# RMS norm and projection on one core: another list schedule for the first six tiles, with earlier and later loads, transposes and casts

The kernel runs on one core of one Trainium2 chip. The metric is device time in microseconds (us) of one execution; lower is better. The kernel before takes 388.32 us (median of three runs, 387.97 to 388.36).

## The reference

```python
# x: 8 x 1024 x 768 f32, gamma: 768, w_qkv: 768 x 2304, eps: 1e-5
rms = np.sqrt(np.mean(x ** 2, axis=-1, keepdims=True) + eps)
x_norm = x / rms * gamma
return np.matmul(x_norm, w_qkv).astype(np.float32)
```

The 8,192 rows of x are 64 tiles of 128 rows. Each tile is multiplied with the whole weight: 6 slices of the contraction (k = 0 to 5) times 2,304 output columns.

## The kernel before

Gamma is folded into the weights as they are cast to bf16 (`conv`). A tile of x is cast, transposed, and multiplied; 1/rms is applied when a result leaves PSUM (`evac`). Tiles 0 to 2 are transposed by TensorE straight from f32 (`trA`, `trB`: slices 0 to 3 and 4 to 5), tile 3 from bf16 (`tr`), and all later ones by the DMA crossbar (`xbar`). In the head (tiles 0 to 5) the weights are still arriving, in 16 pieces. A plan that a list scheduler wrote earlier holds a time for each operation, and only the order within each engine's stream comes out of these times.

```python
PIECES = [(0, 2, 0, 512), (2, 3, 0, 512), (3, 4, 0, 512), ...]   # k0, k1, first column, columns

LOADS = [
    (-9.00, "w", 0), (-8.99, "x", 0), (-8.98, "x", 1), (-8.97, "x", 2), (-8.96, "w", 1),
    (-8.95, "w", 2), (-8.94, "w", 3), (-8.93, "x", 3), (-8.92, "w", 4), (-8.91, "w", 5),
    ...                                          # "t" n: crossbar transpose of tile n
    (15.55, "w", 13), (22.65, "t", 5), ...
]
HEAD_PLAN = [
    (4.98, "conv", 0, 0, "DVE"), (5.46, "conv", 0, 1, "DVE"), (5.94, "trA", 0), (5.98, "stat", 0),
    ...
]
...
    PIECE_BUFS = {(k1 - k0, n): min(4, sum(...)) for k0, k1, _, n in PIECES}   # buffers of a shape
...
    def xbar(t):
        XT[t] = xTp.tile([P, KO, P], bf16, name="xT")
        nc.sync.dma_start_transpose(out=XT[t], in_=XB[t])
...
    at(0.0, idle, 5, NT)          # filler matmuls before the first tile
    at(2.8, gamma_in)
    at(2.81, idle, 6, NT)
...
    for _, _, fn, args in sorted(plan, key=lambda p: p[:2]):
        fn(*args)
```

All loads (but that of gamma), stores and crossbar transposes are issued by SyncE, so they stand in one queue in this order. Tiles 6 to 63 follow from a loop that the change does not touch.

## Time and profile before

| of the kernel before | value |
|---|---|
| time, median of three | 388.32 us |
| span of the profiled execution | 386.2 us |
| TensorE busy | 379.2 us (98%) |
| chain that ended last: share of TensorE | 91% |
| first real matmul starts | 7.53 us |
| tile 5's transpose lands, TensorE goes on | 28.54, 28.58 us |
| last matmul starts | 382.50 us |

Times of the trace count from the span's start. "Landing" is the time at which a load's completion semaphore is full, in the trace's records. TensorE's matmuls overlap, so its real losses are read from start to start: a 512-wide bf16 matmul takes 0.2158 us that way, though the profile shows 0.38 for one alone.

### The profile page before, as it was taken

To read this page: it belongs to the slowest core of one execution; us is meant where nothing else is said; L and a number is where in the kernel's file an instruction comes from. 1 tells how busy PE (TensorE), PEld (TensorE's weight loads), DVE (VectorE), ACT (ScalarE), POOL (GpSimd) and SP (SyncE) were. 2 spreads that over 40 slices of the span, in tenths; PEclk is the share of its full clock that TensorE was granted. 3 is DMA by queue.
4 is the path that set the end of the run, shared out by engine and by line. 5 is a ranking of instruction groups with operands and counts; after the bars stand their busy time and mean duration, and the time that the engine had idled before them with its cause. 6 is when DMAs were issued, how large, how long until landed. Compare 5 with 4: busy or idle time off the path is not lost.

```text
span 386.2 us, 5458 instructions
## 1 busy us (share of the span) xinstructions
PE 379.2 (98%) x1921; PEld 191.5 (50%) x1959; DVE 153.1 (40%) x307; ACT 181.5 (47%) x365; POOL 6.6 (2%) x14
## 2 busy tenths in 40 slices
PE   8999999999999999999999999999999999999996
PEld 4444655455454454554554554554554554554553
DVE  3744433433333344333344333343333343333332
ACT  5752644453544443544444444544444534444532
POOL 0130000000000000000000000000000000000000
PEclk9999999999999999999999999999999999999999
DMA  8999999999999999999999999999999999999995
GB/s 289 391 296 401 401 318 358 321 367 305 331 293 306 310 284 328 294 291 325 276 319 316 298 297 311 299 311 263 297 358 290 306 311 285 290 326 314 282 269 191
DMA packets 89575, 119.91 MB, mean 310 GB/s; under 512 B 52422, under 2 KB 61388, under 8 KB 89548
## 3 DMA queue, kind: packets, MB, share of 16 engines
q1 hardware_dynamic: 89536, 119.56, 101.5%
q8 instruction: 15, 0.25, 0.3%
q14 instruction: 12, 0.10, 0.1%
q10 hardware_dynamic: 12, 0.00, 0.0%
HBM read 32.25 MB, written 75.50 MB: 279 GB/s over the span
## 4 chain that ended last, share of the span: by engine, by line
PE 91%; DMA 6%; issue 1%; DVE 0%; ACT 0%; SPq 0%; DVEq 0%
PE pm L234 91%; DMA x_t<-in_x_dram 3%; DMA w_f<-in_w_qkv_dram 2%; DMA xT<-xb 2%; ACT ot L253 0%; DVE ot L251 0%; DVE xb L174 0%; SPq L160 0%; SPq L155 0%; DVEq L356 0%; ACT w_b L168 0%
## 5 line engine op out<-in xcount | busy, mean ns | idle before, releaser
L234 PE MATMUL pm<-w_b,xT 128*128 128x512 bf16 (+1 forms) x1882 | 372.1, 357 | 2.2 <-DMA xT<-xb 0.2
L234 PEld LDWEIGHTS <-xT 128*128 128x128 bf16 x1920 | 187.7, 98 | 185.6 <-DMA xT<-xb 0.7
L253 ACT ACTIVATE ot<-pm,rstd 128x512 f32<-128x512 f32 (+2 forms) x160 | 102.8, 644 | 192.3 <-PE pm L234 154.5
L251 DVE TENSOR_SCALAR ot<-pm,rstd 128x512 f32<-128x512 f32 (+1 forms) x161 | 111.3, 694 | 201.7 <-PE pm L234 199.1
L185 ACT ACTIVATE sq<-x_t 128x768 bf16<-128x768 f32 x64 | 53.3, 834 | 3.2 <-DMA x_t<-in_x_dram 3.2
L174 DVE CAST xb<-x_t 128x768 bf16<-128x768 f32 x61 | 33.2, 545 | 18.4 <-DMA x_t<-in_x_dram 18.2
L187 ACT ACTIVATE rms<-ssq,eps_sb 128x1 f32<-128x1 f32 x64 | 18.9, 295 | 2.1
L185 ACT ACTIVATION_READ_ACCUMULATOR sq<-x_t 128x1 f32 x64 | 12.2, 191 | 0.0
L166 DVE TENSOR_SCALAR w_b<-w_f,g_sb 128x512 bf16<-128x512 f32 (+1 forms) x16 | 7.7, 499 | 6.3 <-DMA w_f<-in_w_qkv_dram 6.3
L192 DVE RECIPROCAL rstd<-rms 128x1 f32<-128x1 f32 x64 | 9.8, 153 | 0.0
L170 POOL TENSOR_SCALAR w_b<-w_f,g_sb 128x512 bf16<-128x512 f32 (+1 forms) x8 | 5.9, 739 | 23.1 <-DMA w_f<-in_w_qkv_dram 23.1
L286 PE MATMUL pm<-const-float32-0.0 128*128 128x512 bf16 (+1 forms) x14 | 4.8, 491 | 0.8 <-PEq L342 0.8
L168 ACT ACTIVATE w_b<-w_f,g_sb 128x512 bf16<-128x512 f32 (+1 forms) x6 | 3.6, 612 | 2.9 <-DMA w_f<-in_w_qkv_dram 2.9
L212 PE MATMUL pm<-ident_f,x_t 128*128 128x128 f32 x18 | 2.6, 279 | 0.6 <-DMA x_t<-in_x_dram 0.5
L286 PEld LDWEIGHTS <-const-float32-0.0 128*128 128x128 bf16 x14 | 1.5, 123 | 2.6 <-issue 2.6
L212 PEld LDWEIGHTS pm<-ident_f,x_t 128*128 128x128 f32 x18 | 1.9, 140 | 1.6 <-DMA x_t<-in_x_dram 1.3
L176 ACT CAST xT<-pm 128x256 bf16<-128x256 f32 (+1 forms) x5 | 2.2, 454 | 0.2
L142 ACT ACT_TABLE_LOAD x1 | 1.3, 1283 | 1.4 <-PEq L342 1.4
L174 DVE CAST xT<-pm 128x512 bf16<-128x512 f32 x1 | 0.7, 690 | 0.7 <-PE pm L212 0.7
L269 DVE COPY g_sb<-pm 128x6 f32<-128x6 f32 x1 | 0.2, 165 | 1.7 <-PE pm L268 1.7
L268 PEld LDWEIGHTS pm<-ident_f,g 6*128 6x128 f32 x1 | 0.2, 177 | 0.8 <-issue 0.8
L174 DVE COPY xT<-pm 128x768 bf16<-128x768 bf16 x1 | 0.6, 557 | 0.0
(12 smaller groups left out, 2.5 us busy)
## 6 DMA issues: line engine op xcount, KB each, us to landing
out_dram<-ot SPq DMA_DIRECT2D x124, 512.0 KB, 3.9
x_t<-in_x_dram SPq DMA_DIRECT2D x64, 384.0 KB, 4.3
out_dram<-ot SPq DMA_DIRECT2D x64, 128.0 KB, 3.2
w_f<-in_w_qkv_dram SPq DMA_DIRECT2D x10, 512.0 KB, 7.5
out_dram<-ot SPq DMA_DIRECT2D x8, 256.0 KB, 2.0
w_f<-in_w_qkv_dram SPq DMA_DIRECT2D x4, 256.0 KB, 5.8
xT<-xb SPq DMA_TRANSPOSE x60, 4.3
w_f<-in_w_qkv_dram SPq DMA_DIRECT2D x2, 384.0 KB, 5.9
```

What stands on the lines that cost most here:

```text
L166: nc.vector.tensor_scalar(out=o, in0=i, scalar1=g, scalar2=None, op0=mult)
L168: nc.scalar.activation(out=o, in_=i, func=AF.Copy, scale=g, bias=0.0)
L170: nc.gpsimd.tensor_scalar(out=o, in0=i, scalar1=g, scalar2=1.0, op0=mult, op1=mult)
L174: nc.vector.tensor_copy(out=out, in_=in_)
L185: nc.scalar.activation(out=sq, in_=X[t], func=AF.Square, accum_out=ssq)
L187: nc.scalar.activation(out=rms, in_=ssq, func=AF.Sqrt, scale=inv_k, bias=eps_sb)
L192: nc.vector.reciprocal(out=r, in_=RS[t])
L212: nc.tensor.transpose(out=PT[t, h][:, ko - k0, :], in_=X[t][:, ko * P:(ko + 1) * P], identity=ident_f)
L234: nc.tensor.matmul(out=PM[t, n0][:, :nl], lhsT=XT[t][:, ko, :], rhs=w_b[:, ko, n0:n0 + nl], start=(b == 1), stop=(b == KO))
L251: nc.vector.tensor_scalar(out=o[:, :d], in0=pm[:, :d], scalar1=RS[t], scalar2=None, op0=mult)
L253: nc.scalar.activation(out=o[:, d:], in_=pm[:, d:nl], func=AF.Copy, scale=RS[t], bias=0.0)
L286: nc.tensor.matmul(out=wps[:, :nl], lhsT=zeros[:, :P], rhs=zeros[:, :nl], start=True, stop=True)
```

## The change

The intent is a shorter head from another run of the list scheduler. In the head the order on every engine changes, and for some casts, copies and evictions the engine too; the work stays the same but for three filler matmuls. The core of the diff:

```diff
 LOADS = [
     (-9.00, "w", 0), (-8.99, "x", 0), (-8.98, "x", 1), (-8.97, "x", 2), (-8.96, "w", 1),
-    (-8.95, "w", 2), (-8.94, "w", 3), (-8.93, "x", 3), (-8.92, "w", 4), (-8.91, "w", 5),
-    (-8.90, "w", 6), (-8.89, "x", 4), (-8.88, "w", 7), (-8.87, "w", 8), (-8.86, "w", 9),
-    (-8.85, "w", 10), (-8.84, "x", 5), (15.52, "t", 4), (15.53, "w", 11), (15.54, "w", 12),
-    (15.55, "w", 13), (22.65, "t", 5), (22.66, "w", 14), (22.67, "w", 15), (22.68, "x", 6),
-    (22.69, "x", 7),
+    (-8.95, "w", 2), (-8.94, "x", 3), (-8.93, "w", 3), (-8.92, "w", 4), (-8.91, "w", 5),
+    (-8.90, "w", 6), (-8.89, "w", 7), (-8.88, "x", 4), (-8.87, "w", 8), (-8.86, "w", 9),
+    (-8.85, "w", 10), (-8.84, "x", 5), (16.68, "t", 4), (16.69, "w", 11), (16.70, "w", 12),
+    (21.70, "t", 5), (21.71, "w", 13), (21.72, "w", 14), (21.73, "w", 15), (21.74, "x", 6),
+    (21.75, "x", 7),
 ]
 HEAD_PLAN = [
-    (4.98, "conv", 0, 0, "DVE"), (5.46, "conv", 0, 1, "DVE"), (5.94, "trA", 0), (5.98, "stat", 0),
-    (6.81, "trB", 0), (6.95, "cpA", 0, "DVE"), (7.03, "trB", 1), (7.24, "trA", 1),
-    (7.31, "cpB", 0, "ACT"), (7.63, "recip", 0), (7.67, "cpB", 1, "ACT"),
-    (7.69, "mm", 0, 0, "01"), (8.03, "cpA", 1, "ACT"), (8.12, "trB", 2), (8.34, "trA", 2),
...
-    (11.52, "recip", 1), (11.63, "tr", 3), (11.63, "idle", 3), (11.68, "conv", 4, 5, "DVE"),
...
+    (4.98, "conv", 0, 0, "POOL"), (4.98, "conv", 0, 1, "DVE"), (5.94, "trA", 0),
+    (5.98, "stat", 0), (6.81, "trB", 0), (7.03, "trA", 1), (7.17, "cpB", 0, "DVE"),
+    (7.31, "cpA", 0, "ACT"), (7.46, "trB", 1), (7.57, "recip", 0), (7.73, "cpA", 1, "DVE"),
+    (7.93, "trA", 2), (7.97, "stat", 2), (8.36, "mm", 0, 0, "01"), (8.64, "conv", 1, 2, "DVE"),
...
+    (10.74, "mm", 1, 0, "3"), (10.96, "tr", 3), (10.97, "conv", 3, 4, "DVE"),
+    (11.29, "mm", 2, 0, "3"), (11.45, "cp", 3, "DVE"), (11.51, "mm", 0, 0, "4"),
+    (11.64, "conv", 4, 5, "POOL"), ...
 ]
-HEAD_END = 43.99
+HEAD_END = 43.93
```

In SyncE's queue, tile 3's load moves ahead of weight piece 3, tile 4's load behind piece 7, and tile 5's transpose ahead of piece 13.

## The prediction

> **What bounds the kernel now.** I read the page first, then TensorE's waits in the first 48 us, then TensorE and its weight loads in order of time, then the DMA issues and the windows around the crossbar transposes.
>
> ```profile
> PE 379.2 (98%) x1921; PEld 191.5 (50%) x1959; DVE 153.1 (40%) x307; ACT 181.5 (47%) x365; POOL 6.6 (2%) x14
> ...
> PE 91%; DMA 6%; issue 1%; DVE 0%; ACT 0%; SPq 0%; DVEq 0%
> ```
> TensorE is busy 98% of a span of 386.2 us, and the chain that ended last is TensorE for 91%. The chain leaves TensorE only before 28.58 us and in the last 4 us; in between are nothing but groups of up to 63 matmuls with 0.05 us of issue. So the change, all of it in the head, can be worth only what TensorE loses before 28.58.
>
> ```profile
> PE pm L286 <- PEq L342: 0.8, 1, 0.8
> PE pm L212 <- DMA x_t<-in_x_dram: 0.5, 1, 0.5
> PE pm L234 <- DMA xT<-xb: 0.2, 1, 0.2
> ```
> These are all the waits of TensorE there: the start, the first tile of x, and the transpose of tile 5. Matmul ends are modelled, so smaller losses must be read from starts:
>
> ```profile
> 5.84 1.85 PE L212 MATMUL pm<-ident_f,x_t 128*128 128x128 f32 x12 [0.49 <-DMA x_t<-in_x_dram]
> 7.53 0.59 PE L234 MATMUL pm<-w_b,xT 128*128 128x512 bf16 x2
> 7.97 0.82 PE L212 MATMUL pm<-ident_f,x_t 128*128 128x128 f32 x6
> 8.62 2.97 PE L234 MATMUL pm<-w_b,xT 128*128 128x512 bf16 x13
> 11.46 0.51 PE L198 MATMUL pm<-ident,xb 128*128 128x128 bf16 x6
> 11.81 0.34 PE L286 MATMUL pm<-const-float32-0.0 128*128 128x128 bf16 x3
> 12.06 16.35 PE L234 MATMUL pm<-w_b,xT 128*128 128x512 bf16 x73
> 28.58 1.69 PE L234 MATMUL pm<-w_b,xT 128*128 128x512 bf16 x7 [0.17 <-DMA xT<-xb]
> ```
> Start to start in the trace's records, a 512-wide matmul takes 0.2158 us, an f32 transpose 0.109 (0.164 for the first after a wait) and a bf16 transpose 0.056. The 13 matmuls from 8.62 take 2.81 us, so they run gapless to 11.43. From 12.06 the program has 75 matmuls before tile 5 (73 are recorded), 16.19 us, so slots end at 28.25, but the next starts at 28.58. That wait is really 0.33 us, not 0.17.
>
> ```profile
> 26.30:27.30 1.00, 1.00 (x6) 0.49 (x5) 0.49 (x1) 0.68 (x1) 1.00 (x2) 1.00 0.07 25
> ```
> This window has start:end, length, busy time of PE, PEld, DVE, ACT and POOL, granted clock, DMA share and GB/s. Here, in the middle of tile 5's transpose, the DMA engines are almost still. In the packet records 15 of 16 rings have done half the transpose at 26.2 and wait for one that is some 18 packets of 2,048 B behind, at 84 ns each; all go on at 27.67. At 22.25 one engine had moved a 16,384-byte packet of instructions (1.09 us). The transpose, which lands at 28.54, is thus late through the load ahead of it and through one late ring.
>
> **What the Trainium skill says.** "Runtime: NRT & Kernel Launch", Instruction fetch mechanics: instructions are refilled in 16 KiB blocks of 256. The trace agrees: 15 such packets, some 24 us apart. "DMA: Bandwidth & Descriptors", Queues, rings and completion order: each issuing engine has one ring on each of the same 16 engines, with descriptors consumed in ring order. The trace agrees in effect: loads land in issue order, one 512 KB weight piece every 1.35 us and one tile of x every 0.98. "GPSIMD Engine Reference", Elementwise side-by-side: GpSimd was measured 1.96 times as slow as VectorE on an f32 add. Here a 128x512 cast takes 0.69 us on GpSimd (up to 0.99 beside VectorE) and 0.49 on VectorE, so 1.4 to 2 times. "TensorE: Matmul & The Clock Gate", Parts 1 and 4: a clock gate watches a window of about 3.4 us and may not count transposes as work. No trace here shows a drop between 4.6 and 386 us; it is a rival below.
>
> **The change part by part.** I place the new order on the landings and durations above. Loads up to the fourth tile keep their landings: first weight piece 4.83, tiles 0 to 2 at 5.80, 6.78, 7.78, next pieces 8.44 and 9.17. A matmul may start about 0.04 us after what it waits for.
>
> *Start, loses.* TensorE now does 16 transposes before any matmul. The first 12 end at 7.53 as now, but then it needs tile 2, landed at 7.78, where before two matmuls filled that time. It starts at 7.82: 0.29 lost, and 0.055 for the slow first transpose, +0.345 us. First matmul: 7.82 + 0.164 + 3 x 0.109 = 8.32. GpSimd's cast of half the first piece (ready by about 5.9) and ScalarE's copy of tile 0 (6.99 + 0.59 = 7.58) are long done, so moving the cast to GpSimd is worth nothing.
>
> *Middle, gains.* Now, 11.43 to 12.06 holds 6 bf16 transposes (0.346) and 0.29 us of three filler matmuls, the wait for the fourth tile's cast (10.85 to 11.41) and that for the fifth piece's cast, which queues behind it on VectorE. With the fourth tile a piece sooner it lands at 9.17 + 0.98 = 10.16 and its cast ends at 10.74. Counting forward from 8.32: four matmuls to 9.18 (second piece cast by 8.95), two to 9.61, two transposes to 9.83, five matmuls to 10.91, tile 3's transposes at 10.91 (cast ready, 10.78) to 11.25, one matmul to 11.47 (fourth piece, landed 10.82, cast by 11.37). Then eight matmuls while GpSimd casts the fifth piece (11.58 to 12.3 at most 12.6; needed at 13.20), and four more to 14.06. The same point is 14.00 now. So -0.29 us, and start and middle sum to +0.055.
>
> *Up to tile 5, neutral.* From 14.06 TensorE needs each weight piece at these times: sixth 14.06 (both VectorE casts done 13.8), seventh 15.79 and 16.43 (GpSimd 15.3 and at worst 16.2), eighth 17.51 (16.5), ninth 19.24 (19.0 at worst), tenth 20.96 (20.1), eleventh 22.69 (21.7). None is late, but the margins are 0.2 to 1.0 us. Tile 4's transpose is issued about a microsecond later, after a cast ending near 17.1, but still queues behind tile 5's load: landing near 22.4, needed at 23.77.
>
> *Tile 5, gains.* Its transpose now stands ahead of a 512 KB piece instead of behind it, so it lands near 28.54 - 1.35 = 27.2 even with the same late ring. TensorE reaches it at 14.06 + 66 x 0.2158 = 28.30. The wait goes: -0.33 us against a start kept at 28.25 + 0.055. The displaced piece lands near 28.5 and is needed only after 37.
>
> Sum: +0.345 - 0.29 - 0.33 = -0.275. The start at 28.58 becomes 28.30 and the rest is unchanged: 388.32 - 0.28 = 388.04, say 388.05 us. The kernel's own plan shortens by 0.06 us, as its end goes from 43.99 to 43.93; it does not know the late ring.
>
> **Rivals.** (1) *A new wait in the head.* VectorE's 0.04-us margin at tile 3's transposes and the fourth piece (0.1 us) could miss, and GpSimd's pieces could be late if its casts stretch past the 0.99 us seen. For it: seven casts of the first eleven pieces on GpSimd against four. Against: each margin is kept with worst observed durations. It would cost 0.1 to 0.7 us: 388.2 to 388.7. (2) *Tile 5 stays late.* If the fetch or the transpose's own issue (1.58 us after the cast at 22.16) delays it by 1.1 us beyond my estimate, the wait returns: about 388.4. For it: the late ring depends on when TensorE's block is fetched. Against: other transposes land a median 4.3 us after issue, so 26.5 would be possible. (3) *The clock gate closes* in a stretch with transposes alone from 5.35 to 8.32, 2.97 us against 2.18 now; the page's window is longer than either. If it closed for one window, half of 3.4 us lost: about 389.7 (an estimate from that page). (4) *All three losses matter less than the spread* of the three runs, 0.39 us: then nothing is seen, 388.3.
>
> **Range and chances.** The parts give 388.05. The spread (387.97 to 388.36) gives about 0.2 either way, and rivals 1 and 2 push up only: 387.6 to 388.7. A change of 2% is 7.8 us; all TensorE loses between 5.84 and 28.58 is about 1 us, so faster by 2% is excluded but for accident; slower would need several waits at once.
>
> **What would show it right or wrong.** In the changed profile: a pause of about 0.3 us in the f32 transposes before the third tile, first real matmul near 8.3; no filler matmuls and no pause near 11 to 12; the wait for tile 5's transpose gone, its start near 28.3, the transpose landed near 27.2 with a still DMA stretch about 1.3 us earlier than now; TensorE never waiting for GpSimd. The prediction is wrong if waits of TensorE for weight casts appear between 9 and 28 us, if the granted clock dips, or if tile 5's transpose lands after 28.3.

## The result

The changed kernel takes 388.18 us (median of six runs, 387.91 to 388.59), the kernel before 388.25 beside it (six runs, 387.97 to 388.36). The ratio is 1.000, with a 95% interval from 0.9987 to 1.0013. A ratio here is the mean time of one kernel's fast runs over that of the other's fast runs of the same rounds, so it is not quite the ratio of the medians.

The profiled run of the changed kernel took 388.00 us. Its page first (line 236 is line 234 of the kernel before):

```profile
PE 378.8 (98%) x1918; PEld 191.5 (50%) x1956; DVE 153.7 (40%) x309; ACT 179.1 (46%) x360; POOL 8.9 (2%) x17
...
PE 91%; DMA 6%; DVE 1%; issue 1%; SPq 0%; ACT 0%; DVEq 0%
```

TensorE is still the bound. These are its waits in the first 48 us (who waits, for whom, us in total, times, longest):

```profile
PE pm L288 <- PEq L344: 0.8, 1, 0.8
PE pm L214 <- DMA x_t<-in_x_dram: 0.6, 1, 0.6
```

The third line that the kernel before had, the wait for tile 5's transpose, is gone. TensorE in order of time (start, length, operation, count):

```profile
5.85 2.61 PE L214 MATMUL pm<-ident_f,x_t 128*128 128x128 f32 x16 [0.65 <-DMA x_t<-in_x_dram]
8.29 1.46 PE L236 MATMUL pm<-w_b,xT 128*128 128x512 bf16 x6
9.59 0.38 PE L214 MATMUL pm<-ident_f,x_t 128*128 128x128 f32 x2
9.81 1.24 PE L236 MATMUL pm<-w_b,xT 128*128 128x512 bf16 x5
10.89 0.50 PE L200 MATMUL pm<-ident,xb 128*128 128x128 bf16 x6
11.22 21.10 PE L236 MATMUL pm<-w_b,xT 128*128 128x512 bf16 x95
```

The prediction had the first real matmul at 8.32 (it is 8.29), the two transposes at 9.61 (9.59), tile 3's transposes at 10.91 (10.89), and then no pause at all. The last group runs on through the place near 28.3 where tile 5 begins. The weight loads show the pauses of the first tiles more clearly:

```profile
5.85 0.64 PEld L214 LDWEIGHTS pm<-ident_f,x_t 128*128 128x128 f32 x6 [1.14 <-DMA x_t<-in_x_dram]
6.83 0.64 PEld L214 LDWEIGHTS pm<-ident_f,x_t 128*128 128x128 f32 x6 [0.34 <-DMA x_t<-in_x_dram]
7.80 0.42 PEld L214 LDWEIGHTS pm<-ident_f,x_t 128*128 128x128 f32 x4 [0.33 <-DMA x_t<-in_x_dram]
```

The last line is the new wait, for tile 2, which landed at 7.76. Before it, TensorE waits for tile 1 in both kernels.

One thing had not been foreseen. This is the second from 17 to 18 us (start:end, length, busy time of PE, PEld, DVE, ACT and POOL with counts, clock, DMA share, GB/s), in the kernel before and then in the changed one:

```profile
17.00:18.00 1.00, 1.00 (x6) 0.49 (x5) 0.20 (x3) 0.00 (x0) 0.61 (x1) 1.00 1.06 391
```
```profile
17.00:18.00 1.00, 1.00 (x6) 0.48 (x5) 0.26 (x2) 0.91 (x4) 0.08 (x1) 1.00 0.99 264
```

The changed kernel moves 264 instead of 391 GB/s. Its weight piece 9 was issued only at 15.65 us instead of 14.08, because it waited for a buffer that GpSimd had just freed. Tile 5's load therefore landed at 22.03 instead of 21.58, and tile 6's, behind it, 0.46 us later as well. Tile 4's transpose landed at 22.96 and tile 5's at 27.65. TensorE needed them at 23.7 and 28.3, so it didn't wait.

Two seconds of the changed kernel around tile 5's transpose, in the same columns, show that the still stretch of the DMA is there, a little earlier:

```profile
25.00:26.00 1.00, 1.00 (x6) 0.49 (x5) 0.41 (x1) 0.69 (x1) 0.35 (x1) 1.00 2.17 152
26.00:27.00 1.00, 1.00 (x7) 0.41 (x5) 0.54 (x2) 0.00 (x0) 0.64 (x1) 1.00 0.37 86
```

The last matmul starts at 382.18 us instead of 382.50, a gain of 0.32, where 0.28 had been worked out. The two profiled executions, however, differ by 0.20 us in time (388.20 and 388.00), and the medians by 0.07 us only. So part of the gain is lost outside the trace's span: the time holds some 2 us that lie before the first or after the last instruction of the span, 388.20 - 386.19 = 2.01 us in the kernel before and 388.00 - 385.87 = 2.13 in the changed one. The experiments look for the rest in the span; the part outside it is taken up under "What the sum left out".

### The profile page after: what moved, and what is told of

Its sections match the earlier page's. It is cut to its first block, busy times and chain, and to the rows that moved or that the text cites. A ratio compares the mean times of both kernels' runs of the same rounds, so it can differ in the third digit from the quotient of the medians.

```text
span 385.9 us, 5446 instructions
## 1 busy us (share of the span) xinstructions
PE 378.8 (98%) x1918; PEld 191.5 (50%) x1956; DVE 153.7 (40%) x309; ACT 179.1 (46%) x360; POOL 8.9 (2%) x17
## 4 chain that ended last, share of the span: by engine, by line
PE 91%; DMA 6%; DVE 1%; issue 1%; SPq 0%; ACT 0%; DVEq 0%
PE pm L236 91%; DMA x_t<-in_x_dram 4%; DMA w_f<-in_w_qkv_dram 2%; DVE ot L253 0%; DVE w_b L168 0%; SPq L157 0%; DVE xb L176 0%; SPq L162 0%; ACT ot L255 0%; DVEq L253 0%; DVEq L176 0%
## 5 line engine op out<-in xcount | busy, mean ns | idle before, releaser
L255 ACT ACTIVATE ot<-pm,rstd 128x512 f32<-128x512 f32 (+1 forms) x158 | 101.5, 644 | 192.4 <-PE pm L236 146.4
L253 DVE TENSOR_SCALAR ot<-pm,rstd 128x512 f32<-128x512 f32 (+2 forms) x163 | 112.3, 694 | 194.4 <-PE pm L236 193.8
L172 POOL TENSOR_SCALAR w_b<-w_f,g_sb 128x512 bf16<-128x512 f32 (+1 forms) x11 | 8.2, 753 | 21.2 <-DMA w_f<-in_w_qkv_dram 21.2
L168 DVE TENSOR_SCALAR w_b<-w_f,g_sb 128x512 bf16<-128x512 f32 (+1 forms) x15 | 6.3, 447 | 5.0 <-DMA w_f<-in_w_qkv_dram 4.8
L288 PE MATMUL pm<-const-float32-0.0 128*128 128x512 bf16 x11 | 4.3, 547 | 0.8 <-PEq L344 0.8
L170 ACT ACTIVATE w_b<-w_f,g_sb 128x512 bf16<-128x512 f32 (+1 forms) x4 | 2.7, 668 | 1.2 <-DMA w_f<-in_w_qkv_dram 1.1
L178 ACT CAST xT<-pm 128x512 bf16<-128x512 f32 (+1 forms) x4 | 1.8, 470 | 0.5 <-PE pm L214 0.5
L176 DVE CAST xT<-pm 128x256 bf16<-128x256 f32 (+1 forms) x2 | 1.1, 558 | 1.6 <-PE pm L214 1.6
```

The lines of the kernel that those rows point to most:

```text
L168: nc.vector.tensor_scalar(out=o, in0=i, scalar1=g, scalar2=None, op0=mult)
L170: nc.scalar.activation(out=o, in_=i, func=AF.Copy, scale=g, bias=0.0)
L172: nc.gpsimd.tensor_scalar(out=o, in0=i, scalar1=g, scalar2=1.0, op0=mult, op1=mult)
L176: nc.vector.tensor_copy(out=out, in_=in_)
L253: nc.vector.tensor_scalar(out=o[:, :d], in0=pm[:, :d], scalar1=RS[t], scalar2=None, op0=mult)
L255: nc.scalar.activation(out=o[:, d:], in_=pm[:, d:nl], func=AF.Copy, scale=RS[t], bias=0.0)
```

## The experiments

Twelve runs were made, of edited and unedited kernels, in three groups, each beside the kernel before on the same chip (the first group on another chip than the other two). All are correct. Of the kernel before there were 6 runs beside the result, 9 beside the first group (median 388.32) and 12 by the end of the other two groups, which share them (median 388.28; one of the 12 took 390.25).

The table collects what the profiles of all 14 executions show. "Wait" is what TensorE lost there, from start to start. "Last" is the start of the last matmul, and "time" that one execution's.

| profile | tile 2 lands | first real matmul | tile 4 lands (wait) | tile 5 lands (wait) | last | time |
|---|---|---|---|---|---|---|
| before | 7.78 | 7.53 | 22.35 | 28.54 (0.33) | 382.50 | 388.20 |
| before, again | 8.02 | 7.70 | 22.60 | 28.58 (0.17) | 382.54 | 388.24 |
| changed | 7.76 | 8.29 | 22.96 | 27.65 | 382.18 | 388.00 |
| changed, second | 8.40 | 8.94 | 24.72 (0.38) | 27.99 | 383.21 | 389.07 |
| changed, third | 8.07 | 8.61 | 23.43 | 28.12 | 382.50 | 388.31 |
| changed, fourth | 7.62 | 8.16 | 23.04 | 27.75 | 382.04 | 387.89 |
| tile 5 behind piece 13 | 7.63 | 8.17 | 23.35 | 29.40 (1.29) | 383.36 | 389.19 |
| matmuls in front | 7.92 | 7.69 | 23.00 | 27.66 | 382.22 | 388.07 |
| matmuls in front, again | 8.70 | 8.47 | 23.68 | 28.39 | 382.99 | 388.85 |
| and tile 4 later | 8.22 | 7.64 | 23.88 | 28.53 | 382.53 | 388.36 |
| five buffers | 7.58 | 8.12 | 22.24 | 26.95 | 382.00 | 387.83 |
| before, tile 5 ahead | 8.18 | 7.60 | 24.21 (0.38) | 27.54 | 382.93 | 388.55 |
| early instruction packet | 7.94 | 8.48 | 24.96 | 28.27 | 383.52 | 389.35 |
| tile 4 ahead | 7.69 | 8.23 | 21.71 | 27.44 | 383.50 | 389.32 |

### 1. Tile 5's transpose back behind piece 13

```diff
-    (21.70, "t", 5), (21.71, "w", 13), ...
+    (21.70, "w", 13), (21.71, "t", 5), ...
```

> The changed kernel with tile 5's crossbar transpose put back behind the 512 KB weight piece (13). My theory (the place of this transpose in the DMA queue is worth the late gain): it lands about 1.37 us later than in the changed kernel (27.65), near 29.0, TensorE reaches tile 5 at 28.2 and waits about 0.8 us; last matmul 382.18 + 0.8 = 383.0, time about 0.8 us above the changed kernel's 388.18, near 389.0. Rival (its place does not matter, the transpose has slack or the time is set elsewhere): no wait, time within 0.2 us of 388.18.

Measured: 388.95 us (five runs, 388.52 to 389.19), ratio 1.0016 to the kernel before, 95% interval 1.0004 to 1.0029. TensorE in order of time at tile 5:

```profile
29.44 6.86 PE L236 MATMUL pm<-w_b,xT 128*128 128x512 bf16 x31 [1.13 <-DMA xT<-xb]
```

The transpose landed at 29.40 and TensorE lost 1.29 us from start to start, more than the 0.8 expected, as the load of tile 5 was itself 0.43 us later in this execution (22.46). The rival is refuted: the place of this transpose in the queue counts, and in the changed kernel it has to stand ahead of piece 13.

### 2. Tile 0's matmuls in front of tile 2's transposes

```diff
-    (7.93, "trA", 2), (7.97, "stat", 2), (8.36, "mm", 0, 0, "01"), ...
+    (7.93, "trA", 2), (7.97, "stat", 2), (7.90, "mm", 0, 0, "01"), ...
```

> The changed kernel with tile 0's first two matmuls moved in front of the third tile's transposes, where the kernel before had them. My theory (the new order loses about 0.3 us waiting for the third tile): the wait at 7.5 shrinks to under 0.1 us (ScalarE's copy of tile 0 ends at 7.56), but most of it comes back as waits for the second, third and fourth weight piece's casts (about 0.08 + 0.03 + 0.03), so the sixth piece's first matmul moves from 14.03 to about 13.92 and the last matmul from 382.18 to about 382.07: -0.1 us. Rival A (all of it is gained): last matmul near 381.9, -0.25 to -0.3 us. Rival B (order at the start is worth nothing): unchanged.

Measured: 387.93 us (five runs, 387.74 to 388.27), ratio 0.9991, interval 0.9978 to 1.0003. In the profile tile 2 landed 0.16 us later than in the first profile of the changed kernel, so the absolute numbers can't be compared; the rule found in experiment 5 puts the changed kernel with that landing at 382.34, and this one is at 382.22. That is -0.12, as expected, and TensorE lost 0.165 and 0.035 us waiting for casts of weight pieces 1 and 3. Most of the wait for tile 2 thus turns into waits for weights.

### 3. Five buffers for the 512 KB pieces

```diff
-    PIECE_BUFS = {(k1 - k0, n): min(4, sum(...
+    PIECE_BUFS = {(k1 - k0, n): min(5, sum(...
```

> The changed kernel with five buffers instead of four for the 512 KB weight pieces. In the changed kernel piece 9 is issued only at 15.65, when GpSimd frees a buffer, and the DMA queue runs short of work near 17 to 18 us; tile 5's x lands at 22.03 instead of 21.58. My theory (this shortage is real but hidden): with five buffers x of tile 5 lands near 21.55, tile 5's transpose near 27.2, and the last matmul stays at 382.18 +- 0.05. Rival (the spread of the changed kernel's runs, 387.9 to 388.6 in two clusters, comes from tile 5's transpose missing its margin of 0.54 us in some runs): then all runs of this one lie in the lower cluster, 387.9 to 388.0, and none above 388.2.

Measured: 388.37 us (five runs, 387.83 to 388.55), ratio 1.0002, interval 0.9988 to 1.0016. Tile 5's load landed at 21.43 and its transpose at 26.95: the shortage of loads near 17 us comes from the buffers and was hidden. The last matmul starts at 382.00, outside the 382.18 +- 0.05 expected, because tile 2 landed 0.18 us earlier; it follows the first one by 373.88 us, as in the changed kernel (373.89). The rival is refuted, as four of the five runs lie above 388.2 although tile 5's transpose has 1.1 us to spare in the profile. Something else makes the longer runs.

### 4. The kernel before with tile 5's transpose ahead of piece 13 alone

```diff
-    (15.55, "w", 13), (22.65, "t", 5), (22.66, "w", 14), ...
+    (22.64, "t", 5), (22.65, "w", 13), (22.66, "w", 14), ...
```

> The kernel before with one part of the change alone: tile 5's transpose issued ahead of weight piece 13. My theory: it lands near 27.2 instead of 28.54, the wait of 0.33 us before tile 5 goes, everything earlier in the head stays as before, last matmul 382.50 - 0.33 = 382.17, time about 387.9, so this one line is worth as much as the whole change. Rival (the gain of the late part depends on the other changes): wait stays, time 388.25.

Measured: 388.24 us (five runs, 387.93 to 388.55), ratio 0.9998, interval 0.9986 to 1.0011. The wait at tile 5 is gone, with a landing at 27.54, but no time is gained in the median: the 387.9 of my theory is missed. In the profiled run, the longest of the five, TensorE waits somewhere new. Here are its second group of real matmuls, its waits from 10 to 48 us, and the DMA in the window before:

```profile
9.01 2.97 PE L234 MATMUL pm<-w_b,xT 128*128 128x512 bf16 x13
```
```profile
PE pm L234 <- DMA xT<-xb: 0.2, 1, 0.2
```
```profile
22.50:23.50 1.00, 1.00 (x7) 0.44 (x5) 0.00 (x0) 0.66 (x3) 0.00 (x0) 1.00 0.06 7
```

The wait is 0.38 us from start to start, at tile 4, whose transpose landed at 24.21 instead of 22.35. For a second, the 16 DMA engines moved 7 GB/s. The 16,384-byte instruction packet had started at 21.78, while tile 4's transpose was still under way. In the first profile it came at 22.25, when that transpose had moved its last bytes. So the late ring that the prediction saw at tile 5 can also hit tile 4; tile 5's transpose then had no still stretch (its longest packet took 56 ns). The new wait is only a part of the late end. In the first profile the last matmul starts 373.55 us after the second group, plus the waits (8.62 + 373.55 + 0.33 = 382.50). Here it is 9.01 + 373.55 + 0.38 = 382.94, against 382.93 measured: with the wait at tile 5 gone, the late start (9.01 instead of 8.62, with tile 2 landing at 8.18 instead of 7.78) counts in full.

### 5. The changed kernel again, twice

> The changed kernel again, unedited, for a second profile. Its timed runs lie in two clusters (387.9 to 388.0 and 388.4 to 388.6), and the one profile is of the lower. Theory (a late ring: TensorE's 16,384-byte instruction packet near 22 us falls, in some runs, before or inside tile 4's transpose, whose second half then waits): if this run is over 388.25 it shows tile 4's transpose landing after 23.8 instead of 22.96, TensorE waiting 0.3 us or more before tile 4; if it is under 388.1 it shows no such wait. Rival 1 (the clusters come from when the first tiles of x land): the upper cluster has tiles 0 to 2 landing 0.3 us later and no wait at tile 4. Rival 2 (tile 5's transpose misses its margin): the wait is at tile 5.

> As the run before: the changed kernel unedited, a third profile, read in the same way. Late-ring theory: over 388.25 goes with tile 4's transpose landing after 23.8; rival 1: with later first tiles; rival 2: with a wait at tile 5.

Measured: 389.07 and 388.31 us. TensorE in order of time in the slower of the two:

```profile
8.45 0.66 PE L214 MATMUL pm<-ident_f,x_t 128*128 128x128 f32 x4 [0.73 <-DMA x_t<-in_x_dram]
...
24.77 7.51 PE L236 MATMUL pm<-w_b,xT 128*128 128x512 bf16 x34 [0.22 <-DMA xT<-xb]
```

and in the other, where no later wait is listed:

```profile
8.12 0.66 PE L214 MATMUL pm<-ident_f,x_t 128*128 128x128 f32 x4 [0.34 <-DMA x_t<-in_x_dram]
```

Both have tile 2 late, and one has tile 4 late on top. The late-ring theory fits the first only in part. Its instruction packet started at 22.68, when the last packets of tile 4's transpose were done and not during them; 15 of the 16 completion counts had come by 23.25, the last one at 24.72. The theory fails for the second, which is over 388.25 without a wait at tile 4. Rival 1, the first loads, explains 0.64 of the 1.03 us by which the first run's last matmul is late, and all 0.32 us of the second's. There is a rule in it: in all four profiles of the unedited changed kernel, the first real matmul starts 0.53 or 0.54 us after tile 2 lands, and the last matmul 373.89 us after that, plus the wait at tile 4 where there is one.

### 6. An earlier instruction packet

```diff
-    at(0.0, idle, 5, NT)
+    at(0.0, idle, 20, P)
...
-    at(2.81, idle, 6, NT)
+    at(2.81, idle, 24, P)
```

> The changed kernel with its 11 filler matmuls of 512 columns before the first tile made 44 of 128 columns: the same TensorE time, 66 instructions more, so that TensorE's first instruction packet comes some 33 x 0.2158 = 7 us earlier, near 15 us, before both transposes. Late-ring theory: the late ring catches up in the short supply of loads near 17 us, tile 5's transpose has no still stretch and lands near 26.3 instead of 27.65, no run waits at tile 4, all five runs 387.9 to 388.1. Rival (clusters come from the first loads): two clusters as before, whatever the transposes do.

Measured: 389.69 us (six runs, 388.38 to 390.54), ratio 1.0028, interval 1.0007 to 1.0049. Both theories missed the time. The packet did move, to 15.85, and one part of the late-ring theory held: tile 5's transpose has no still stretch. Its 768 packets moved from 27.02 to 27.74 us, none over 19 ns, where in the unedited changed kernel 19 of them take over 1 us. Instead tile 4's transpose, the first after the packet, was held up (from 21.18 to 24.37, 12 of its packets taking over 1 us). So the still stretch at tile 5 goes with the instruction packet, here and in experiment 4. But the early packet made the loads of weights late, which had been on time, and TensorE now waits for casts:

```profile
PE pm L236 <- POOL w_b L172: 0.5, 2, 0.3
PE pm L236 <- DVE w_b L168: 0.2, 1, 0.2
```

From start to start these three waits are 0.47, 0.35 and 0.34 us. The ring did not catch up near 17 us: weight piece 9 landed at 20.37 instead of 19.63, and tile 5's load at 24.09 instead of 22.03. A late ring costs most where the loads have least to spare.

### 7. Tile 4's transpose ahead of tile 5's load

```diff
-    (-8.85, "w", 10), (-8.84, "x", 5), (16.68, "t", 4), (16.69, "w", 11), ...
+    (-8.85, "w", 10), (16.68, "t", 4), (16.685, "x", 5), (16.69, "w", 11), ...
```

> The changed kernel with tile 4's transpose issued ahead of tile 5's load instead of behind it; the instruction order of TensorE is unchanged. Late-ring theory: it lands near 22.2 and is over before the instruction packet in most runs, and even with a late ring (1.4 us) it lands by 23.6 against the 23.7 at which TensorE needs it; the upper cluster goes, all runs 387.9 to 388.1. Rival: clusters stay (median near 388.2).

Measured: 389.53 us (six runs, 389.32 to 390.17), ratio 1.0033, interval 1.0015 to 1.0051. Both the theory (387.9 to 388.1) and its rival (388.2) are missed. The transpose is early (21.71) and still the kernel is slower. TensorE's longest wait, and VectorE in order of time at that place:

```profile
PE pm L236 <- DVE ot L253: 1.2, 1, 1.2
```
```profile
34.37 0.56 DVE L176 CAST xb<-x_t 128x768 bf16<-128x768 f32 x1 [3.90 <-DMA x_t<-in_x_dram]
34.85 0.75 DVE L253 TENSOR_SCALAR ot<-pm,rstd 128x512 f32<-128x512 f32 x1
```

Tile 5's load landed at 24.07 and, behind it in the queue, tile 6's at 34.35 instead of 32.24. VectorE stands 3.9 us at the cast of tile 6. Behind it in VectorE's order is the eviction of tile 5's first result, and TensorE needs that PSUM buffer at 34.25 us. It gets it at 35.65. The loads of the head thus have a second deadline that no wait in the two first profiles shows: TensorE went on 1.30 us after tile 6 had landed (35.65 - 34.35; cast and eviction take 0.56 and 0.75 us), so tile 6 has to land before about 34.25 - 1.30 = 32.95. The first profile of the changed kernel (32.24) passes that with about 0.7 us.

### 8. The changed kernel, five rounds

> The changed kernel unedited, five rounds beside the kernel before, because the gain of 0.28 us predicted from one profile is 0.32 us in the profiles and 0.07 us in the medians. My theory (the gain is real for tiles 0 to 2 landing as in the first profiles, but every 0.1 us by which tile 2 lands later than 7.49 costs the changed kernel 0.1 us, while the kernel before is free until 7.93; in the profiles tile 2 landed at 7.58 to 8.40): median 388.1 to 388.4, within 0.15 us of the kernel before; in the profile, last matmul = first real matmul + 373.9 + waits at tiles 4 and 5. Rival (the first six runs were unlucky): median 388.0, 0.28 us under the kernel before.

Measured: 388.48 us (six runs, 387.89 to 389.20), ratio 1.0006, interval 0.9988 to 1.0024. The fourth profile fits the rule: tile 2 at 7.62, first real matmul at 8.16, last at 382.04, and 8.16 + 373.89 = 382.05. The rival (an unlucky first six) is not borne out. My range for the median (388.1 to 388.4) is missed by 0.08, and the 0.15 us to the kernel before by 0.05 (388.48 and 388.28).

### 9. The kernel before again

> The kernel before unedited, for a second profile. My theory: last matmul = start of its second group of real matmuls (8.62 in the first profile) + 373.55 + waits of the middle and at tile 5 (0.33 in the first profile), and the time is near 388.3. Rival: a wait in another place than the first profile showed.

Measured: 388.24 us. TensorE in order of time:

```profile
7.70 0.59 PE L234 MATMUL pm<-w_b,xT 128*128 128x512 bf16 x2
...
8.84 2.97 PE L234 MATMUL pm<-w_b,xT 128*128 128x512 bf16 x13
...
12.27 19.98 PE L234 MATMUL pm<-w_b,xT 128*128 128x512 bf16 x91
```

These starts are 0.17, 0.22 and 0.21 us later than in the first profile (7.53, 8.62 and 12.06). Yet no pause is listed at tile 5 and the last matmul is only 0.04 us later, because the wait at tile 5 shrank from 0.33 to 0.17. The rule (start of the second group + 373.55 + waits) holds with that wait: 8.84 + 373.55 + 0.17 = 382.56. What matters more is the other reading: in both profiles the last matmul starts 353.96 us after tile 5's transpose lands. The transpose sets the end. In experiment 1, too, the last matmul starts 353.96 us after that landing. A start 0.22 us late cost this kernel nothing by itself, and by the wait of the first profile up to 0.33 us would not (an estimate).

### 10. Matmuls in front, again, and with tile 4 later

> The changed kernel with tile 0's first two matmuls back in front of the third tile's transposes, once more, beside the unedited one on the same chip. My theory (free of the wait for tile 2 until 7.93, and of the filler and of tile 5's wait): median 387.95, 0.2 to 0.4 us under both kernels. Rival (its first five runs were lucky): 388.2.

Measured: 388.47 us (six runs, 388.07 to 388.85), ratio 1.000, interval 0.9984 to 1.0016. This misses 387.95. The first five runs were lucky in part; on two chips, the median of the 11 runs is 388.17. In the profile tile 2 landed at 8.70, the latest of all. The rule would put the changed kernel at 383.12, and this kernel is at 382.99, again 0.13 us earlier. The second run has the edit of experiment 2 and this one:

```diff
-    (26.40, "mm", 4, 1024, "0123"), (26.56, "evac", 4, 512, "DVE"), (27.27, "mm", 2, 1024, "5"),
-    (27.31, "conv", 12, 3, "POOL"), (27.48, "mm", 3, 1024, "45"), ...
+    (26.40, "mm", 4, 1024, "0123"), (26.56, "evac", 4, 512, "DVE"), (23.70, "mm", 2, 1024, "5"),
+    (27.31, "conv", 12, 3, "POOL"), (23.75, "mm", 3, 1024, "45"), ...
```

> The run before with one thing more: three matmuls of tiles 2 and 3 moved in front of tile 4, so that TensorE reaches tile 4 at 24.3 instead of 23.65. My theory (tile 4's transpose is late by over a microsecond in some runs, 24.2 and 24.7 seen): median as the run before, 387.9, and no run over 388.2. Rival (late transposes of tile 4 are not what makes slow runs): spread as the run before.

Measured: 388.16 us (six runs, 387.86 to 388.51), ratio 0.9993, interval 0.9976 to 1.0010. Two of six runs are over 388.2, against my expectation of none, and the median misses 387.9. Its profile has tile 2 at 8.22 and tile 4 at 23.88, without a wait at either transpose. It has the lowest median of its group, but neither it nor the one before it is clearly faster than the kernel before: both intervals contain 1.

## Why the prediction was right

The time on record was 388.05, from 387.6 to 388.7; measured were 388.18 and, later, 388.48. Over all 14 runs of the unedited changed kernel the median is 388.34, over all 27 of the kernel before 388.29 (these pool chips and calls, so they are a check and not a verdict). The range took in the kernel before as well, so the time alone says little: what it forecast, a gain of 0.28 us, is found in the trace and not in the times. The parts in turn:

**Start.** "0.29 lost, and 0.055 for the slow first transpose, +0.345 us": confirmed. In the profile the two losses are 0.26 and 0.055, because tile 2 landed 0.02 us earlier. That moving half of the first cast to GpSimd is worth nothing was not tried by itself; the profile has that cast done at 5.98, and it is not needed before 8.29.

**Middle.** "-0.29 us" is confirmed: from 8.29 to tile 5 no loss between two starts exceeds 0.03 us, and tile 3's cast ended at 10.68, where 10.74 was worked out.

**Up to tile 5.** "None is late" held, but one term was missing: the buffer for weight piece 9. It made the two transposes land 0.56 and 0.45 us later than reckoned (22.96 and 27.65 against 22.4 and 27.2). Experiment 3 shows that this is the cause and that it was hidden.

**Tile 5.** "The wait goes: -0.33 us" is confirmed by the profile and, from the other side, by experiment 1. The sum, -0.275, compares with -0.32 from the first profile of each kernel. One reading was off without effect: at 26.2 us the rings that were ahead had begun about two thirds of the transpose (507 of its 768 packets), not half; it is the late ring that moved about 24 of its 48 packets before all went on.

**Rivals.** Rival 1 (waits for casts) did not come in the unedited changed kernel. Rival 4 (the spread hides the gain) is what the medians show. Rival 2 did not come at tile 5, but tile 4's transpose was completed late in one of four profiles of the changed kernel, for 0.38 us. The clock gate (rival 3) did not close.

**What the sum left out.** Two things. The first lies outside the span. The step "the rest is unchanged" does not hold for the time: the runs of the experiments and of the result list their time and their span (to 0.1 us), and time less span is 1.89 to 2.09 us (mean 1.97) in the 21 runs of the kernel before that list both, and 2.10 to 2.19 (mean 2.15) in the 14 of the changed kernel. On the second chip alone the means are 1.99 and 2.15. The edited kernels go with the one that they came from: experiment 4 has 1.90 to 2.03, the others 2.11 to 2.21. From the last matmul to the end of the span it is 3.68 to 3.70 us in all 14 profiles. So about 0.18 us of the gain is lost before the first or after the last instruction, whatever the loads do. No run here shows why.

The second is that it took the loads of one execution as given. Tile 2 landed between 7.58 and 8.70 us in the 14 profiles, with a median of 7.93. The kernel before waits for tile 5's transpose anyway, and that wait takes up a late start; both its profiles end 353.96 us after that landing. The changed kernel has no wait left that could do so: all four of its profiles follow the landing of tile 2 to within 0.01 us, plus tile 4's wait in one. Setting the two equal, 382.52 - 373.89 - 0.53 = 8.10, so the change gains in the span where tile 2 lands before about 8.10. After that it loses, but little: by experiment 4 (9.01 - 8.18 = 0.83) the kernel before then follows its start too, at 0.83 + 373.55 = 374.38 us after the landing against 373.89 + 0.53 = 374.42. At the median landing the gain in the span is 0.17 us, and without the 0.18 us nothing is left of it (estimates from these numbers, without tile 4's wait). That is what the medians show. It stays argued: the part outside the span is measured in each of these runs, but no run holds tile 2's landing fixed.

The spread fits: the changed kernel's 14 runs go from 387.89 to 389.20, while 24 of the 27 runs of the kernel before lie between 387.97 and 388.54 (the others at 388.75, 388.82 and 390.25). Why the first loads land at different times stays open.

## What to carry to other kernels

A wait late in a start-up phase can be slack for everything ahead of it; removing it gains only what the earlier steps do not then pass on, and makes the time follow the first loads. Take more than one profile before crediting a gain of 0.1%, compare which event the end follows, and check that what the span gains is gained in the time as well. Reordering one queue moves deadlines that no wait shows yet, as the casts in experiment 6 and the PSUM buffer in experiment 7 did.

## What the Trainium skill lacked or had wrong

- "Advanced Engine Details and Errata", X-Bar Transpose (TRN2), says that transpose DMAs are as fast as regular DMAs. Here it is slower even without a late ring: in experiment 6 tile 5's transpose moved its 768 packets of 256 bytes in 0.72 us, 273 GB/s, right after a microsecond in which loads moved 389 GB/s (26 to 27 us).
- "DMA: Bandwidth & Descriptors", DMA Transpose (X-bar), doesn't say what the packet records suggest: partway through a transpose the rings that are ahead wait for a late one, and all go on together. At tile 5 of the kernel before, 23 packets of 256 bytes took 1,434 to 1,459 ns instead of 18 and ended together near 27.7 us, and the DMA moved 25 GB/s for a microsecond; in experiment 4, 7 GB/s.
- "Runtime: NRT & Kernel Launch", Instruction fetch mechanics, calls the cost of a new instruction block mostly hidden. The 16,384-byte packet near 22 us took 0.93 to 1.15 us of a DMA engine in 12 of the 14 profiles. With the packet at 15.85 us, casts that waited for weights cost TensorE 0.47, 0.35 and 0.34 us, and the kernel ran at a ratio of 1.0028.
- No page gives a figure for the spread of the first loads: the third tile of x, the fourth load in the queue, landed between 7.58 and 8.70 us in 14 executions.
- "TensorE: Matmul & The Clock Gate", Part 1, leaves the time of the warm-up open within a window, and the runs agree: the full clock was granted between 3.73 and 6.89 us after the span's start. In the run with 6.89, f32 transposes took 0.213 us from start to start instead of 0.109. Part 4 says that transposes don't count as busy in the same way. No closing of the gate was seen in the 2.4 us of transposes and waits before the first real matmul, but that is shorter than the window of about 3.4 us in Part 1, so it is no test.
- No page has that two programs with the same work can differ in the time outside the span: time less span is 1.89 to 2.09 us in the runs of the kernel before and 2.10 to 2.19 in those of the changed one.
